# A two-block network on one core: bias tables at tile 9, the shift's chunks in another ring, and the mixers' matmuls of 128 and of 64 rows in separate groups

## The chip, the cores and the metric

The kernel runs on one core of one Trainium2 chip, as one program launch. The metric is the device time of that launch in microseconds (us); runs are summed up by their median. The engines are TensorE (PE in the profile; its weight loads are PEld), VectorE (DVE), ScalarE (ACT), GpSimd (POOL) and SyncE (SP), whose queue issues nearly all DMAs, strictly in order.

## The reference, cut to what matters

The input is 256 tokens of width 1024, all in float32. The first block runs two layers. Each layer is

```
mod = (silu(c) @ ada_w[l] + ada_b[l]).reshape(B, 3, 3, 1, D)       # shift, scale, gate of three sublayers
h = rms_norm(x, g0) * (1 + scale0) + shift0
x = x + 0.5 * gate0 * swiglu(h, ffn1_w13[l], ffn1_w2[l])           # width 2816
h = rms_norm(x, g1) * (1 + scale1) + shift1
x = x + gate1 * (four mixers of width 256 on h @ w_in[l] + b_in[l], joined, @ w_out[l])
x = x + 0.5 * gate2 * swiglu(rms_norm(x, g2) * (1 + scale2) + shift2, ffn2_w13[l], ffn2_w2[l])
```

The four mixers are a sparse attention (with a table of relative position biases, `t5_table`), a short convolution, a gated delta rule and an mLSTM. The last two work in chunks of 64 tokens. For the delta rule, with state S of each of four heads,

```
v_new = u_c - w_c @ S
o     = qd_c @ S + qk_c @ v_new
S     = S * gt_c + kd_c.T @ v_new
```

and for the mLSTM the output is a sum of `q_c @ C` (the state) and `s @ v_c` (inside the chunk), divided by a normaliser. A second block of two layers (a recurrent and attention mixer, a retention mixer, and two wide MLPs) follows; the change does not touch it.

## The kernel before, in words

Every large weight lies in one DRAM stream, cut into chunks of 128 rows by 1024 columns (512 KB). `raw` (L135) loads a chunk with one DMA on SP's queue into a ring of buffers; `weights` (L153) then splits it into a rounded part `whi` on ScalarE (L150) and a remainder `wlo` on VectorE or GpSimd (L151), and each product is three fp32r matmuls (L167 to L169). The weights' ring `wraw` has four buffers, `whi` and `wlo` four each, so loads can run about four feature tiles' halves ahead of the splits and those about as far ahead of TensorE.

The Tile framework decides the order of instructions on each engine by simulating the program's timeline at build time; an instruction may be placed earlier than its place in the text. Two things pin the order. `tc.issue_after(x)` puts an instruction behind `x` on its engine; and while `self.in_order` is set, `raw` pins each load behind the last SP instruction of the text, so that SP issues in the order of the text. `in_order` holds in the first FFN from its beginning through its last feature tile.

The first FFN of the first layer, `ffn` (L368) with `begin` (L2220) and `side` (L2336), goes like this:

- `begin` handles feature tiles 0 to 5 together ("wide": eight steps over k, each with a column of x scaled by `mod`), then tiles 6 and 7, one product for each half z. The wide chunks and those of tiles 6 and 7 use the ring `g` of 16 places. The scale vector's eight chunks of the modulation weights are loaded into the ring `wada` (three buffers) and reduced on VectorE (`ada_parts`, L233: one multiply and sum over 1024 columns, then a small correction). The shift vector's eight chunks are loaded by `shift_part` (L2253), also into `wada`, and reduced on TensorE by narrow matmuls (`strips`, L252). Four further steps of `ada_parts` are taken by `next(more)` (L2297), one for each half of tiles 6 and 7.
- The loop over tiles 8 to 21 loads two chunks for each tile, multiplies, scales by `rstd` (`se`, L384), applies SiLU and the gate (`sb`, L392), splits the result into `g` (L150 on ScalarE, L151 on GpSimd), and takes one step of `ada_parts`, which loads one chunk and reduces it.
- From tile `SIDE` (12) on, each tile also takes a step of `side`: first four loads (1104 KB of constants, an identity of 64 KB, a one-hot table of 49.5 KB and the bias table), four matmuls of 33 rows into the two PSUM banks that the shift's sums also use, and four ScalarE copies that make `bv` (`bias_tables`, L463, L474, L475); a tile later `skew` (L477) stores `bv` to DRAM on SP (L484); two tiles later it loads it back skewed as `bt` (L487); two tiles later VectorE copies parts of it to `bc` (L494). These SP instructions are pinned into the order of the text.
- The second product of the FFN runs over eight output tiles m, each in three cuts of k (`W2_CUTS`, 24 chunks in all). At the head of each m it takes two steps of `ada_parts`. There, SP is no longer pinned, and no VectorE instruction of `ada_parts` is pinned anywhere.

In the mixers, a planner (`weave`, L521) interleaves the streams of the four mixers and the output product by start times and paces. In `gdn` (L835), each of four chunks computes for each head `qd @ S` (L981, 128 rows: a state of two heads' width, padded with zeros) and `Qm @ v_new` (L982, 64 rows) into one PSUM tile, head after head. In `mlstm` (L1018), each half t computes for each head and chunk `qT @ C` into `pa` (L1141, 128 rows) and `sT @ v1` into `pb` (L1143, 64 rows), in turn. Each of these fp32 matmuls is two records in the trace.

Of the kernel before, what the change touches and what calls it, by code (L numbers as in the profile page):

```python
# [12 lines left out]
ALU = mybir.AluOpType  # L13
# [15 lines left out]
WIDE = 6  # L29
FIRST = 8  # L30
PLACES = 16
SIDE = 12
W2_CUTS = ((0, 8), (8, 15), (15, 22))


# [136 lines left out]
class Block1(Core):  # L172
# [50 lines left out]
    def ada_parts(self, pool, rows, name="wada", bufs=3):  # L223

        nc = self.nc
        for l, j in rows:
            t = self.mod[l, j] = self.keep1.tile([P, 8], F32, name=f"mod{l}_{j}")
            o = self.col_at[f"adab{l}"][0] + 8 * j
            s, kind = divmod(j, 3)
            for m in range(8):  # L230
                w = self.raw(f"ada{l}_{j}_{m}", pool, name, bufs)
                c, b = t[:, m:m + 1], self.cols[:, o + m:o + m + 1]
                nc.vector.scalar_tensor_tensor(w, w, 1.0, self.cond, op0=ALU.mult, op1=ALU.mult, accum_out=c)  # L233
                if kind == 1:
                    g = self.col(f"g{l}_{s}")
                    if m == 0:

                        bg = pool.tile([P, 8], F32, name="bg", bufs=2)
                        nc.vector.scalar_tensor_tensor(bg, self.cols[:, o:o + 8], 1.0, g, op0=ALU.add, op1=ALU.mult)
                    nc.vector.scalar_tensor_tensor(c, c, g[:, m:m + 1], bg[:, m:m + 1], op0=ALU.mult, op1=ALU.add)  # L240
                elif kind == 2 and s != 1:
                    nc.vector.tensor_scalar(c, c, b, 0.5, op0=ALU.add, op1=ALU.mult)
                else:
                    nc.vector.tensor_tensor(c, c, b, op=ALU.add)
                yield
# [122 lines left out]
    def ffn(self, l, s, ada1, ada2, begin=None, side=None):  # L368
        nc, tc = self.nc, self.tc
        psum = Banks(self.pp, acc="bbccdd", st="xy", acc2="ddy", late="dd")  # L370
        with tc.tile_pool(name=f"fh{l}_{s}", bufs=1) as hp:
# [26 lines left out]
            if begin:  # L398

                m0 = FIRST  # L400
                self.in_order = True
                steps = self.ada_parts(hp, ada1 + ada2)
                late, extra = begin(psum, hp, steps)
                self.in_parts = True
                sides = side(psum, hp)
            else:
                steps = self.ada(hp, ada1)
# [33 lines left out]
            self.h = [(a[:, 0:TN], b[:, 0:TN]) for a, b in zip(*([v[:, k] for k in range(KD)] for v in (self.vhi, self.vlo)))]  # L441
            for m in range(KD):
                ps = psum.tile([P, T], F32, name="acc2", bufs=3)
                if begin:
                    for _ in range(2):
                        next(steps, None)
                else:
                    for _ in ada2:
                        next(steps)
                for k0, k1 in W2_CUTS:  # L450
                    w = self.weights(f"w2_{l}_{s}_{m}_{k0}")
                    for k in range(k0, k1):
                        self.mm(ps, w, g[k], slice((k - k0) * P, (k - k0 + 1) * P), k == 0, k == FT - 1)
                self.add_out(m, ps, self.mod[l, 3 * s + 2], (l, 1) if s == 0 else (1, 0) if l == 0 else None)
                if begin and m == 5:

                    hi, lo = self.early
                    self.split(self.mod[l, 3][:, :, None].to_broadcast([P, KD, 2]), hi[:, :, T:], lo[:, :, T:])
# [18 lines left out]
    def skew(self, dr):  # L477


        nc = self.nc  # L480
        self.bt = self.keep1.tile([P, 4, T], F32, name="bt")
        self.bc = self.keep1.tile([P, 2, 4, 16], F32, name="bc")
        d = dr.tile([P, 4, 384], F32, name="bdram")
        nc.sync.dma_start(d, self.bv)  # L484
        yield
        yield
        nc.sync.dma_start(self.bt, bass.AP(tensor=d.tensor, offset=d.offset + 127, ap=[[1535, P], [384, 4], [1, T]]))  # L487
        nc.gpsimd.memset(self.bc, NEG)
        yield
        yield  # L490
        for t in range(2):
            n = 7 if t == 0 else 15
            o = 31 + 128 * (1 - t)
            nc.vector.tensor_copy(self.bc[:, t, :, 0:n], self.bt[:, :, o:o + 16 * (n - 1) + 1:16])  # L494
# [340 lines left out]
    def gdn(self):  # L835
# [129 lines left out]
        for ck in range(4):  # L965
            t, q = divmod(ck, 2)
            s = slice(64 * q, 64 * q + 64)
            tk = slice(64 * ck, 64 * ck + 64)
            if ck:
                ps = big([P, 4, 64])  # L970
                for hh in range(4):
                    nc.tensor.matmul(ps[s, hh], wT[hh % 2][:, t, q, hh // 2], S[:, hh // 2], start=True, stop=True)
                nc.vector.tensor_tensor(vn[s, t], u[s, t], ps[s], op=ALU.subtract)
                vc = vn
            else:
                vc = u
            yield
            ps = big([P, 4, 64])
            for hh in range(4):
                if ck:  # L980
                    nc.tensor.matmul(ps[s, hh], qd[hh % 2][:, hh // 2, tk], S[:, hh // 2], start=True, stop=False)  # L981
                nc.tensor.matmul(ps[s, hh], Qm[s, t, hh], vc[s, t, hh], start=not ck, stop=True)  # L982
            nc.scalar.activation(o[s, t], ps[s], AF.Copy)
            if ck == 3:
                break
            ps = big([P, 2, 64])
            for hh in range(4):
                z = slice(64 * (hh % 2), 64 * (hh % 2) + 64)
                nc.tensor.matmul(ps[z, hh // 2], kd[s, t, hh], vc[s, t, hh], start=True, stop=True)
            Sn = self.mx.tile([P, 2, 64], F32, name="cS", bufs=2)  # L990
            if ck:
                for f in range(2):
                    nc.vector.scalar_tensor_tensor(Sn[:, f], S[:, f], eg[:, f, 64 * ck + 63:64 * ck + 64], ps[:, f],
                                                   op0=ALU.mult, op1=ALU.add)
            else:
                nc.vector.tensor_copy(Sn, ps)
            S = Sn
            yield
# [19 lines left out]
    def mlstm(self):  # L1018
# [115 lines left out]
        for t in range(2):  # L1134
            pa = big([P, 4, 65])
            pb = big([P, 4, 65])
            for hh in range(4):
                for q in range(2):
                    s = slice(64 * q, 64 * q + 64)
                    tk = slice(t * P + 64 * q, t * P + 64 * q + 64)  # L1140
                    nc.tensor.matmul(pa[s, hh], qT[hh % 2][:, hh // 2, tk], C[:, 2 * t + q, hh // 2],  # L1141
                                     start=True, stop=True)
                    nc.tensor.matmul(pb[s, hh], sT[s, t, hh], v1[s, t, hh], start=True, stop=True)  # L1143
            yield
            n1 = self.mx.tile([P, 4, 65], F32, name="dn1", bufs=1)
# [1068 lines left out]
def first(b, z_ap, c_ap, t5_ap, onehot_ap, cst_ap, where):  # L2214
    nc, tc = b.nc, b.tc
    with ExitStack() as ctx:
        b.open1(ctx)
        dr = ctx.enter_context(tc.tile_pool(name="bd", bufs=1, space=DRAM))

        def begin(psum, pool, more):  # L2220

            b.condition(c_ap)
            steps = b.ada_parts(pool, [(0, 1)])
# [29 lines left out]
            def shift_part(h, q):  # L2253

                if q == 0:
                    sums[h] = psum.tile([P, 2, 256], F32, name="st")
                w = b.raw(f"ada0_0_{4 * h + q}", pool, "wada", 3)
                a = [w[:, k % 4 * 256:(k % 4 + 1) * 256] for k in range(KD)]
                b.strips(sums[h][:, q // 2], cond, a, range(4 * (q % 2), 4 * (q % 2) + 4))

# [29 lines left out]
            for m in range(WIDE, FIRST):  # L2290
                t = pool.tile([P, 2, T], F32, name="se2", bufs=FIRST)
                for z in range(2):
# [1 line left out]
                    ps = psum.tile([P, T], F32, name="acc")  # L2294
                    b.product(ps, b.weights(f"w13_0_0_{m}_{z}", False, raws[-1]), [(a[:, 0:T], c[:, 0:T]) for a, c in b.u])
                    nc.vector.tensor_tensor(t[:, z], ps, b.rstd, op=ALU.mult)
                    next(more)  # L2297
                    if m == WIDE and z == 0:
                        finish(0)
                    for q in ((0,), (1,), (2, 3), ())[2 * (m - WIDE) + z]:  # L2300
# [35 lines left out]
        def side(psum, pool):  # L2336
            nc.sync.dma_start(b.ident, b.ident_ap)
            b.constants1(cst_ap, where)
            b.bias_tables(t5_ap, onehot_ap, psum, pool)
            yield  # L2340
            yield from b.skew(dr)

        for l in range(2):
# [64 lines left out]
```

## Time and profile before

| what | value |
|---|---|
| three runs | 1999.63, 1990.77, 1995.83 us; median 1995.83 us |
| profiled execution | 2000.48 us, its span 1998.6 us, mean granted clock 0.975 |
| TensorE, weight loads | 96 % and 91 % of the span |
| VectorE, ScalarE, GpSimd | 75 %, 51 %, 28 % of the span |
| chain that ended last | TensorE 85 %, VectorE 7 %, DMA 3 % |
| DMA | 384.21 MB, mean 192 GB/s |

The first block takes the first 1100 us or so of the span: the first FFN of layer 0 from 0 to 245, its mixers from there to 455, the second FFN to 850, and the mixers of layer 1 to about 1050. A row of the timeline gives the start, the length, the engine, the source line and what is written from what; rows of the same kind are merged, with their count as x2 and so on, and a bracket gives the idle time before and what ended it. A matmul's length covers its fill and drain and overlaps the next one, so a rate is read from the distance of starts. PEclk is the clock that TensorE was granted: 1.00 is 2.4 GHz and 0.50 is 1.2 GHz, and a figure between is a mixture over the stretch.

### The profile page before, as it was taken

To read this page: it belongs to the slowest core of one execution; us is meant where nothing else is said; L and a number is where in the kernel's file an instruction comes from. 1 tells how busy PE (TensorE), PEld (TensorE's weight loads), DVE (VectorE), ACT (ScalarE), POOL (GpSimd) and SP (SyncE) were. 2 spreads that over 40 slices of the span, in tenths; PEclk is the share of its full clock that TensorE was granted. 3 is DMA by queue.
4 is the path that set the end of the run, shared out by engine and by line. 5 is a ranking of instruction groups with operands and counts; after the bars stand their busy time and mean duration, and the time that the engine had idled before them with its cause. 6 is when DMAs were issued, how large, how long until landed. Compare 5 with 4: busy or idle time off the path is not lost.

```text
span 1998.6 us, 40143 instructions
## 1 busy us (share of the span) xinstructions
PE 1926.8 (96%) x16031; PEld 1827.9 (91%) x16031; DVE 1501.9 (75%) x2693; ACT 1009.7 (51%) x1712; POOL 566.0 (28%) x474
## 2 busy tenths in 40 slices
PE   7989988999999999989999999999999999999998
PEld 7889977889999999977889999878999999999998
DVE  7669688678997999987547665678985686568954
ACT  4445454345454555454335554565654465556643
POOL 1143341104431443351104440313421122243302
PEclk9999988999999999989989999989999999999999
DMA  8758648326787788845116766424455544446562
GB/s 332 271 218 316 209 131 261 109 87 240 286 279 259 264 287 280 304 142 176 63 35 210 221 189 194 142 80 136 159 190 166 194 131 156 150 158 195 174 202 95
DMA packets 108808, 384.21 MB, mean 192 GB/s; under 512 B 12075, under 2 KB 14668, under 8 KB 108364
## 3 DMA queue, kind: packets, MB, share of 16 engines
q1 hardware_dynamic: 108620, 381.64, 57.0%
q8 instruction: 126, 2.06, 0.4%
q14 instruction: 62, 0.51, 0.1%
HBM read 379.76 MB, written 1.84 MB: 191 GB/s over the span
## 4 chain that ended last, share of the span: by engine, by line
PE 85%; DVE 7%; DMA 3%; issue 2%; ACT 1%; POOL 1%; SPq 0%; POOLq 0%; ACTq 0%; DVEq 0%
PE acc L167 23%; PE acc L169 23%; PE acc L168 23%; DMA wraw<-in_stream_dram 2%; DVE wlo L151 1%; PE b L2007 1%; DVE wada L233 1%; PE pa L1284 1%; ACT whi L150 1%; PE pc L924 1%; PE pa L1311 1%; DVE vlo L292 1%; DMA g<-in_stream_dram 1%; PE pc L942 1%; PE acc L733 1%
## 5 line engine op out<-in xcount | busy, mean ns | idle before, releaser
L150 ACT ACTIVATE whi<-wraw 128x1024 fp32r<-128x1024 f32 (+2 forms) x546 | 563.5, 1036 | 466.3 <-PE acc L168 323.9
L151 DVE TENSOR_TENSOR wlo<-wraw,whi 128x1024 fp32r<-128x1024 f32 (+1 forms) x471 | 594.9, 1266 | 204.1 <-ACT whi L150 197.5
L167 PE MATMUL acc<-vhi,whi 128*128 128x258 f32 (+3 forms) x2176 | 621.7, 288 | 21.2 <-ACT whi L150 17.6
L168 PE MATMUL acc<-vlo,whi 128*128 128x258 f32 (+3 forms) x2176 | 620.8, 286 | 2.4 <-DVE vlo L292 2.4
L169 PE MATMUL acc<-vhi,wlo 128*128 128x258 f32 (+3 forms) x2176 | 615.6, 286 | 3.1 <-DVE wlo L151 3.0
L167 PEld LDWEIGHTS acc<-vhi,whi 128*128 128x128 f32 x2176 | 413.1, 191 | 28.9 <-ACT whi L150 19.5
L168 PEld LDWEIGHTS acc<-vlo,whi 128*128 128x128 f32 x2176 | 416.0, 191 | 5.3 <-DVE vlo L292 3.2
L169 PEld LDWEIGHTS acc<-vhi,wlo 128*128 128x128 f32 x2176 | 411.6, 190 | 6.9 <-DVE wlo L151 4.0
L151 POOL TENSOR_TENSOR wlo<-wraw,whi 128x1024 fp32r<-128x1024 f32 (+1 forms) x75 | 190.2, 2540 | 271.2 <-ACT whi L150 261.3
L168 PE MATMUL acc<-g,whi 128*128 128x256 f32 x704 | 199.2, 283 | 0.8 <-POOL g L151 0.8
L167 PE MATMUL acc<-g,whi 128*128 128x256 f32 x704 | 198.4, 282 | 1.3 <-ACT g L150 1.3
L169 PE MATMUL acc<-g,wlo 128*128 128x256 f32 x704 | 199.1, 283 | 0.0
L167 PE MATMUL acc<-hhi,whi 128*128 128x256 f32 (+1 forms) x576 | 169.7, 298 | 6.4 <-ACT whi L150 2.8
L169 PE MATMUL acc<-hhi,wlo 128*128 128x256 f32 (+1 forms) x576 | 168.7, 295 | 0.0
L168 PE MATMUL acc<-hlo,whi 128*128 128x256 f32 (+1 forms) x576 | 168.3, 293 | 0.0
L151 POOL TENSOR_TENSOR g<-sb,g 128x256 fp32r<-128x256 f32 x88 | 106.1, 1209 | 161.7 <-ACT g L150 150.5
L167 PE MATMUL acc<-ghi,whi 128*128 128x272 f32 (+1 forms) x512 | 146.4, 286 | 0.0
L169 PE MATMUL acc<-ghi,wlo 128*128 128x272 f32 (+1 forms) x512 | 145.9, 285 | 0.0
L168 PE MATMUL acc<-glo,whi 128*128 128x272 f32 (+1 forms) x512 | 145.7, 285 | 0.0
L167 PEld LDWEIGHTS acc<-g,whi 128*128 128x128 f32 x704 | 133.5, 190 | 1.5 <-ACT g L150 1.5
L168 PEld LDWEIGHTS acc<-g,whi 128*128 128x128 f32 x704 | 133.1, 189 | 1.0 <-POOL g L151 1.0
L169 PEld LDWEIGHTS acc<-g,wlo 128*128 128x128 f32 x704 | 133.2, 189 | 0.0
(631 smaller groups left out, 3610.9 us busy)
## 6 DMA issues: line engine op xcount, KB each, us to landing
wraw<-in_stream_dram SPq DMA_DIRECT2D x502, 512.0 KB, 4.0
wada<-in_stream_dram SPq DMA_DIRECT2D x128, 512.0 KB, 4.7
wraw<-in_stream_dram SPq DMA_DIRECT2D x64, 448.0 KB, 4.5
g<-in_stream_dram SPq DMA_DIRECT2D x16, 512.0 KB, 7.5
wraw<-in_stream_dram SPq DMA_DIRECT2D x8, 384.0 KB, 3.1
cst<-in_cst_dram SPq DMA_DIRECT2D x1, 1104.0 KB, 7.9
z<-in_z_dram SPq DMA_DIRECT2D x8, 136.0 KB, 6.9
rows<-in_rows_dram SPq DMA_DIRECT2D x2, 532.0 KB, 4.7
```

What stands on the lines that cost most here:

```text
L150: self.nc.scalar.activation(hi, src, AF.Copy)
L151: (self.nc.gpsimd if pool else self.nc.vector).tensor_tensor(lo, src, hi.bitcast(F32), op=ALU.subtract)
L167: nc.tensor.matmul(ps, wh[:, kw], xh, start=start, stop=False)
L168: nc.tensor.matmul(ps, wh[:, kw], xl, start=False, stop=False)
L169: nc.tensor.matmul(ps, wl[:, kw], xh, start=False, stop=stop)
L233: nc.vector.scalar_tensor_tensor(w, w, 1.0, self.cond, op0=ALU.mult, op1=ALU.mult, accum_out=c)
L292: nc.vector.scalar_tensor_tensor(lo[:, m, 0:T], self.x[m], A[:, m:m + 1], hi[:, m, 0:T].bitcast(F32), op0=ALU.mult, op1=ALU.subtract)
L733: nc.tensor.matmul(ps[t], hh[:, tk], wh[:, kw], start=k == 0, stop=False)
L924: nc.tensor.matmul(ps[s, hh], M[s, t, hh], c["eye"][s] if v == 1 else de[t][s, 0, hh], start=True, stop=True)
L942: nc.tensor.matmul(ps[s, 1, hh], p1[t][s, hh], de[t][s, 1, hh], start=True, stop=True)
L1284: nc.tensor.matmul(ps[:, 0:n], qn[z, hh // 2, t * P:(t + 1) * P], keys[b, hh % 2][:, 0:n], start=True, stop=True)
L1311: nc.tensor.matmul(ps[:, hh], PT[hh][:, kb], v[:, kb, b], start=kb == 0, stop=kb == t)
```

## The change

Six edits, in three groups.

1. Bias tables: `SIDE` becomes 9. `side` waits four tiles between making the tables and storing them, so the store stands at tile 13 as before; the load back stands at tile 14 instead of 15, and the copies to `bc` at tile 18 instead of 17.
2. Modulation: the shift's eight chunks are loaded into the ring `wraw` instead of `wada`. The four steps at tiles 6 and 7 go; the second product takes 18 steps instead of 14, one ahead of each cut but the first of an m (and one ahead of that too for m = 2 and 5) instead of two at the head of each m. While `in_parts` is set (tile 8 to the end of the FFN), the VectorE reduction of a step is pinned behind the last VectorE instruction of the text.
3. Mixers: `gdn` issues the four heads' `qd @ S` first and then the four `Qm @ v_new`, with one start and one stop for the bank; `mlstm` issues all eight `qT @ C` and then all eight `sT @ v1`.

```diff
-SIDE = 12
+SIDE = 9
@@ ada_parts
-                nc.vector.scalar_tensor_tensor(w, w, 1.0, self.cond, op0=ALU.mult, op1=ALU.mult, accum_out=c)
+                with self.tc.issue_after(self.last(mybir.EngineType.DVE)) if self.in_parts else ExitStack():
+                    nc.vector.scalar_tensor_tensor(w, w, 1.0, self.cond, op0=ALU.mult, op1=ALU.mult, accum_out=c)
@@ ffn
-                late, extra = begin(psum, hp, steps)
+                late, extra = begin(psum, hp)
@@ ffn, second product
-                if begin:
-                    for _ in range(2):
+                for _ in () if begin else ada2:
+                    next(steps)
+                for k0, k1 in W2_CUTS:
+                    if begin and (k0 or m in (2, 5)):
                         next(steps, None)
-                else:
-                    for _ in ada2:
-                        next(steps)
-                for k0, k1 in W2_CUTS:
                     w = self.weights(f"w2_{l}_{s}_{m}_{k0}")
@@ skew
         nc.sync.dma_start(d, self.bv)
         yield
-        yield
         nc.sync.dma_start(self.bt, bass.AP(tensor=d.tensor, offset=d.offset + 127, ap=[[1535, P], [384, 4], [1, T]]))
         nc.gpsimd.memset(self.bc, NEG)
-        yield
-        yield
+        for _ in range(4):
+            yield
@@ gdn
             ps = big([P, 4, 64])
+            for hh in range(4) if ck else ():
+                nc.tensor.matmul(ps[s, hh], qd[hh % 2][:, hh // 2, tk], S[:, hh // 2], start=hh == 0, stop=False)
             for hh in range(4):
-                if ck:
-                    nc.tensor.matmul(ps[s, hh], qd[hh % 2][:, hh // 2, tk], S[:, hh // 2], start=True, stop=False)
-                nc.tensor.matmul(ps[s, hh], Qm[s, t, hh], vc[s, t, hh], start=not ck, stop=True)
+                nc.tensor.matmul(ps[s, hh], Qm[s, t, hh], vc[s, t, hh], start=not ck, stop=not ck or hh == 3)
@@ mlstm
                     nc.tensor.matmul(pa[s, hh], qT[hh % 2][:, hh // 2, tk], C[:, 2 * t + q, hh // 2],
                                      start=True, stop=True)
+            for hh in range(4):
+                for q in range(2):
+                    s = slice(64 * q, 64 * q + 64)
                     nc.tensor.matmul(pb[s, hh], sT[s, t, hh], v1[s, t, hh], start=True, stop=True)
@@ begin, shift_part
-                w = b.raw(f"ada0_0_{4 * h + q}", pool, "wada", 3)
+                w = b.raw(f"ada0_0_{4 * h + q}", b.wp, "wraw", WRAW)
@@ begin, tiles 6 and 7
-                    next(more)
@@ side
             b.bias_tables(t5_ap, onehot_ap, psum, pool)
-            yield
+            for _ in range(4):
+                yield
             yield from b.skew(dr)
```

## Rows read from the trace of the kernel before

**Rows 1.** The page, busy time of each engine.
```profile
PE 1926.8 (96%) x16031; PEld 1827.9 (91%) x16031; DVE 1501.9 (75%) x2693; ACT 1009.7 (51%) x1712; POOL 566.0 (28%) x474
```

**Rows 2.** Windows: PE, PEld, DVE, ACT, POOL busy (records), PEclk, DMA share, GB/s.
```profile
70.00:80.00 10.00, 10.00 (x60) 7.72 (x61) 6.85 (x13) 5.20 (x7) 0.45 (x1) 0.72 0.95 370
...
120.00:130.00 10.00, 4.32 (x27) 3.45 (x26) 3.65 (x8) 3.58 (x8) 1.40 (x2) 0.84 0.79 286
130.00:140.00 10.00, 9.54 (x68) 9.36 (x68) 9.39 (x14) 5.08 (x8) 2.39 (x1) 0.82 1.04 403
...
150.00:160.00 10.00, 10.00 (x86) 10.00 (x85) 9.94 (x15) 5.02 (x11) 6.84 (x4) 1.00 0.80 291
...
180.00:190.00 10.00, 7.90 (x58) 7.49 (x57) 10.00 (x18) 6.59 (x11) 2.87 (x2) 0.91 0.91 303
190.00:200.00 10.00, 10.00 (x79) 10.00 (x79) 9.37 (x18) 4.78 (x8) 0.27 (x1) 0.92 1.00 385
```

**Rows 3.** Waits of SP's DMA queue, 0 to 130: total us, times, longest.
```profile
SPq L484 <- ACT bv L475: 22.4, 1, 22.4
...
SPq L140 <- PE st L252: 16.6, 6, 5.8
```

**Rows 4.** Timeline of SP's queue: start us, us, line, tile, count.
```profile
61.05 0.43 SPq L140 DMA_DIRECT2D g<-in_stream_dram  x1
...
92.39 6.54 SPq L140 DMA_DIRECT2D wraw<-in_stream_dram  x2
121.43 0.33 SPq L484 DMA_DIRECT2D bdram<-bv  x1
...
125.70 0.38 SPq L487 DMA_DIRECT2D bt<-bdram  x1
```

**Rows 5.** Timeline of PE where it waited in the first FFN.
```profile
68.03 0.39 PE L167 MATMUL acc<-vhi,whi 128*128 128x256 f32 x1 [1.48 <-ACT whi L150]
...
129.38 0.58 PE L167 MATMUL acc<-vhi,whi 128*128 128x258 f32 x1 [5.68 <-ACT whi L150]
```

**Rows 6.** Timeline of DVE at the FFN's second product.
```profile
185.80 0.47 DVE L392 SCALAR_TENSOR_TENSOR sb<-se,sh 128x256 f32<-128x256 f32 x1
```

**Rows 7.** DVE's groups by form, 178 to 246: count, busy us, mean ns, idle before.
```profile
L151 DVE TENSOR_TENSOR wlo<-wraw,whi 128x896 fp32r<-128x896 f32 x16 | 18.4, 1153 | 7.2 <-ACT whi L150 7.1
L233 DVE SCALAR_TENSOR_TENSOR wada<-wada,cond 128x1024 f32<-128x1024 f32 x12 | 15.1, 1257 | 0.0
...
L292 DVE SCALAR_TENSOR_TENSOR vlo<-z,mod,vhi 128x256 fp32r<-128x256 f32 x7 | 6.6, 945 | 0.9 <-ACT vhi L291 0.9
```

**Rows 8.** Timeline of PE in layer 0's mixers.
```profile
415.28 0.69 PE L1141 MATMUL pd<-dC,dqT 128*64 128x65 f32 x16
...
421.29 0.68 PE L972 MATMUL pc<-cS,cwT 128*64 128x64 f32 x8
...
422.96 0.68 PE L1143 MATMUL pd<-dv,dsT 64*64 64x65 f32 x16
...
425.05 0.33 PE L982 MATMUL pc<-cvn,csegi 64*64 64x64 f32 x2
425.30 0.33 PE L981 MATMUL pc<-cS,cqd 128*64 128x64 f32 x2
```

**Rows 9.** PE in layer 1's mixers: timeline; windows of both layers, as rows 2.
```profile
1009.83 0.33 PE L1141 MATMUL pd<-dC,dqT 128*64 128x65 f32 x2
...
400.00:450.00 50.00, 49.98 (x530) 42.86 (x530) 35.21 (x101) 24.32 (x63) 2.50 (x3) 1.00 0.29 88
...
1014.30:1031.50 17.20, 17.20 (x103) 14.03 (x102) 6.33 (x24) 4.40 (x12) 1.00 (x1) 0.50 0.01 1
```

**Rows 10.** Groups by form of DVE and POOL, 130 to 178, columns as rows 7.
```profile
L392 DVE SCALAR_TENSOR_TENSOR sb<-se,sh 128x256 f32<-128x256 f32 x6 | 7.0, 1168 | 0.3 <-ACT sh L421 0.3
...
L151 POOL TENSOR_TENSOR wlo<-wraw,whi 128x1024 fp32r<-128x1024 f32 x4 | 12.3, 3085 | 7.8 <-ACT whi L150 7.7
L151 POOL TENSOR_TENSOR g<-sb,g 128x256 fp32r<-128x256 f32 x8 | 11.8, 1489 | 17.2 <-ACT sh L421 11.2 <-ACT g L150 6.0
```

More of the change, by code (lines that the diff above doesn't have):

```diff
@@ L2218, in first, with begin @@
         dr = ctx.enter_context(tc.tile_pool(name="bd", bufs=1, space=DRAM))
-        def begin(psum, pool, more):
+        def begin(psum, pool):
             b.condition(c_ap)
```

## The prediction

> **What bounds the kernel now.** I read the page first: TensorE is busy 96% of the span and nothing else comes near [rows 1]. So a microsecond counts only where TensorE waits, or runs at its lower clock, or takes longer for a matmul than it must. Next I read the windows of the first FFN, since four of the six edits are there. Three stretches stand out [rows 2]: 70 to 80 has a granted clock of 0.72, 120 to 140 has 5.7 us of idle TensorE and clocks of 0.84 and 0.82, and 180 to 200 has 2.1 us of idle and 0.91 and 0.92. Then the waits of SP's queue over the same time [rows 3]: one wait of 22.4 us, the bias tables' store for the copies that make `bv`, and 16.6 us in six waits for the strips' matmuls (L252), which free the places of the shift's chunks. The timelines of SP and TensorE tie these to the stalls [rows 4, 5]. Last I read TensorE in both mixers for what matmuls of 128 and of 64 rows cost side by side [rows 8, 9].
>
> **The change part by part.**
>
> Shift's chunks in `wraw` (A). Before, a shift chunk holds a place of `wada` until TensorE has run its strips, and the next load of that ring, with all that stands behind it on SP, waits. Tile 7's last weights stand behind such a wait and are issued at 61.05 [rows 4]; TensorE idles 1.48 us for them until 68.03 [rows 5]. Then the clock is low: 0.72 over 10 us is 5.6 us at 1.2 GHz and the rest at 2.4, and in those 5.6 half the work, 2.8 us, is lost. In the new text the only waits of this kind ahead of tile 8 are those of the last four shift chunks for the strips of the first four, which TensorE runs long before; the four wada loads of tiles 6 and 7 are gone as well. A is 1.5 + 2.8 = 4.3. What is late next: tile 8's and 9's loads now wait for the strips of the last four chunks, which TensorE must run ahead of tile 8 anyway. Bounds 0 (such a load takes the place of the stall) to 5.
>
> Bias tables (B). SP issues tile 13's weights by 98.9 and then stands at the store until 121.43 [rows 4], with every later weight load behind it. TensorE lives on its lead of 16.7 us (22.4 less the idle 5.68), stops at 123.70 and waits until 129.38 [rows 5]. Idle 5.7; 0.82 in 130 to 140 is 3.6 us at the low level, 1.8 lost; 0.7 for the slow start before 130 and the 0.46 of idle behind it. B is 8.2. In the new text the tables come behind tile 9. Tiles 10 to 13 are 48 matmuls each, 5.8 us at some 0.12 (86 in 10 us at full clock [rows 2]), and the tables themselves some 4 us, so tile 9 ended at about 123.7 - 23 - 4 = 96 to 97, and `bv` is ready between 98 and 104 in old times: SP waits 0 to 6 us, well inside the lead. The moved step issues the same four loads, four matmuls and four ScalarE copies three tiles earlier; on SP its 1.2 MB pass ahead of the weights of tiles 10 to 12, of which TensorE needs the first some 20 us later. The load back stands one tile behind the store, which took at most 4.3 us to land (121.43 to 125.70); that wait too lies inside the lead. At tile 9 the tables share two banks with the late shift columns; with nothing placed between, TensorE would wait up to 4 us. Bounds 4 to 9.
>
> Steps in the second product (C). From 180 to 190 VectorE is busy without a gap [rows 2], because reductions belonging to the second product's heads are placed early; so the last tile's `sb` runs only at 185.80 [rows 6], and TensorE loses 2.1 of idle, and by 0.91 and 0.92 3.4 us at the low level, 1.7. Pinned in the text's order, those reductions no longer pass `sb`: +3.8. Against that, the second product has 18 steps instead of 14. Its sum on VectorE [rows 7]: 24 x 1.15 for `wlo`, 18 x (1.26 + 0.2 of small ones), 8 x 0.95 for `vlo`, 8 updates of x at 0.47 (an operation of the form and size of rows 6) are 65 us, while TensorE's 8 x 22 x 3 matmuls are 62 to 64 at some 0.12. VectorE is at the bound there, and I charge 2.3. C is 1.5, bounds -7 to 4. In rows 7 `vlo` takes 0.95 where the like-sized `sb` of rows 6 takes 0.47; `wlo` is hardly stretched. The Trainium skill, "SBUF — State Buffer", Who interferes with whom, says why it can be worse: a VectorE instruction with two SBUF inputs and a GpSimd one that reads SBUF shut each other out for a whole instruction. By the row the sum is 65; if by the rule each of the eight `vlo` waited for a whole GpSimd instruction of 1.5 us [rows 10] it would be some 8 us more and C about -6, an estimate that the bounds hold.
>
> Delta rule (D). In turn, a block of two records starts every 0.26 us (425.05 to 425.30); eight such blocks a chunk are 2.06. In one group, eight records of 128 rows take 0.68 at most, and sixteen of 64 rows 0.68, so eight take 0.4 [rows 8]; together 1.08. Part of the first block stands apart already. I take 0.8 a chunk; three chunks in two layers give 4.9, bounds 2.5 to 5.8.
>
> mLSTM (E). In layer 0 the timeline shows L1141 and L1143 in groups already [rows 8]: nothing to win. In layer 1 the first half alternates sixteen blocks from 1009.83 on [rows 9], 4.1 us at 0.26 each; in two groups 0.69 + 0.68 = 1.4. E is 2.75, bounds 0 to 3.
>
> The clock behind it (F). Right behind that alternation, the granted clock is 0.50 from 1014.3 to 1031.5 while TensorE never idles [rows 9]; at most half of it, 8.6 us, is lost. In layer 0, where the same steps run in groups, the clock is 1.00 from 400 to 450 [rows 9]. I take 4, bounds -7 (a fall in layer 0 instead) to 8.6.
>
> The sum is 4.3 + 8.2 + 1.5 + 4.9 + 2.75 + 4 = 25.7, say 26 us. Against the profiled execution's 2000.5 that is 1974.3. That execution lies 4.7 above the median of the runs, so the forecast is 1995.8 - 26 = 1970.
>
> **The rivals.**
>
> VectorE gives part of it back. The second product is VectorE's: if its 24 `wlo` and 18 steps wait for each other as pinned and their sum grows from 65 to 74 (each of them stretched by a fifth of a microsecond), TensorE waits 11 there: 1996 - (26 - 1.5) + 11 = 1982. For: rows 7. Against: loads and splits run ahead, and 7 us of VectorE's idle there were waits for ScalarE.
>
> The regrouping doesn't do what it says. The order is placed anew, and layer 0 shows that it departs from the text: L1143 was moved apart there. If the placement splits the groups again, or what is saved only exposes VectorE's chains in the mixers, D, E and F are nothing: 1996 - 14 = 1982. Against: TensorE does not idle in either stretch.
>
> Slower: VectorE falls behind in tiles 8 to 21. A reduction pinned behind `sb` can no longer fill VectorE's wait for ScalarE's SiLU. VectorE needs 1.5 `wlo` at 1.2, two `se` at 0.4, `sb` and a step, 4.6 us a tile, against TensorE's 5.8, but it is stretched by GpSimd: `sb` took 1.17 on average here, not 0.47 [rows 6, 10]. If all of GpSimd's 3 us a tile (1.49 and half of 3.09) blocked VectorE, a tile would be 7.6: 1.8 x 14 = 25 us, and the waits bring clock falls of 2.8 each (as behind 68.03, A), say seven: 20. 1996 - 25 + 45 = 2016. It decides from 5.8 us of VectorE a tile. Against: with that stretching, TensorE was busy 10.00 of 10 at 150 to 160 [rows 2]. The rule of the Trainium skill named under C is what would make this happen; for `sb` the trace agrees with it.
>
> **How the numbers follow.** The forecast has 0.63, the two partial ones 0.16 and 0.13, the slower one 0.08. About 0.5%, 10 us, is what a measurement of this kernel can tell from no change, so faster begins below 1986. Faster: 0.61 + 0.10 + 0.10 = 0.81; slower: 0.07; the rest, 0.12, lies within. The range runs from the sum of all upper bounds, 35 (1961), to the partial rivals at 1982, each widened by the spread of the runs, some 5 us to either side: 1955 to 1988. That leaves out the slower case and the edges, some 2 in 10.
>
> **What would show it.** A: no idle of TensorE and clock 1.00 from 60 to 80. B: SP's wait at the store under 6 us; no idle at tile 14. C: `sb` of tile 21 within 3 us of its matmuls, and no TensorE waits for `wlo` later in the second product. D, E: L981 in runs of eight records, L1141 of sixteen in both layers. F: clock 1.00 through layer 1's mLSTM. It is wrong if the mixers' clock falls elsewhere, or if TensorE waits for `wlo` from tile 8 on.

## The result, and the profile after

The changed kernel takes 1972.02 us (median of 7 runs, 1969.46 to 1983.29), the kernel before 1995.83 (7 runs, 1990.77 to 1999.63). The ratio is 0.9894, 95% interval 0.9868 to 0.9920, so faster, by some 21 us (24 by the medians). The forecast was 1970. The profiled execution took 1972.02 us itself, with a span of 1970.2. The total came out near the forecast; its parts did not, and most of what follows is about that.

Page of the changed kernel, busy time of each engine, as [rows 1]:

```profile
PE 1906.0 (97%) x16031; PEld 1811.7 (92%) x16031; DVE 1498.1 (76%) x2693; ACT 1009.2 (51%) x1712; POOL 566.2 (29%) x474
```

Windows of the changed kernel, columns as [rows 2]:

```profile
70.00:80.00 10.00, 10.00 (x65) 6.46 (x64) 4.16 (x4) 3.79 (x7) 2.39 (x1) 1.00 0.84 330
120.00:130.00 10.00, 10.00 (x86) 10.00 (x85) 9.69 (x15) 6.58 (x13) 8.87 (x5) 1.00 0.62 230
130.00:140.00 10.00, 10.00 (x86) 10.00 (x85) 7.94 (x12) 3.74 (x8) 4.52 (x3) 1.00 0.72 265
170.00:180.00 10.00, 8.11 (x65) 7.69 (x64) 9.70 (x18) 6.41 (x10) 2.41 (x2) 1.00 0.93 315
190.00:200.00 10.00, 10.00 (x86) 10.00 (x85) 10.00 (x16) 4.58 (x7) 1.67 (x2) 1.00 0.96 354
```

The stalls of 70 to 80 and 120 to 140 are gone, and the clock is full there. The idle time at the end of the first product is not gone: TensorE is busy 8.11 of 10 in 170 to 180, where the same place before had 7.90 [rows 2].

Waits and timeline of SP's queue, as [rows 3, 4]:

```profile
SPq L140 <- PE st L253: 23.3, 5, 7.5
SPq L483 <- ACT bv L474: 6.1, 1, 6.1
```

```profile
104.98 0.33 SPq L483 DMA_DIRECT2D bdram<-bv  x1
...
108.42 0.43 SPq L485 DMA_DIRECT2D bt<-bdram  x1
```

The store waits 6.1 us instead of 22.4, just above the 0 to 6 forecast, and the load back follows 3.4 us later. The strips still hold SP for 23.3 us, more than the 16.6 before, but TensorE no longer waits behind them.

TensorE in both layers' mixers, as [rows 8, 9]:

```profile
418.61 0.68 PE L970 MATMUL pc<-cS,cwT 128*64 128x64 f32 x8
419.13 0.63 PE L978 MATMUL pc<-cS,cqd 128*64 128x64 f32 x8
...
996.07 0.69 PE L1139 MATMUL pd<-dC,dqT 128*64 128x65 f32 x16
996.68 0.68 PE L1144 MATMUL pd<-dv,dsT 64*64 64x65 f32 x16
```

The groups are there: sixteen records and sixteen records where sixteen blocks of two took turns. From 985 to 1060 the granted clock is 1.00, with no stretch at 0.50.

One reading serves all that follows. Each run lists its time and its mean granted clock. Time times clock is the least that the run would have taken with the clock at its upper level throughout; the rest is what the low level cost at most, since idle time at the low level would not have shrunk. Before, 48 runs: 1951.2 and 42.3. After, 13 runs of two measurements: 1942.0 and 29.6. So 9.2 us of the gain are work or idle time that went, and 12.7 are clock. By the forecast's terms it should have been 15.4 and 10.3 (clock: 2.8 of A, 1.8 of B, 1.7 of C, 4 of F).

```
kernel                   runs  mean us  time x clock   rest
before                    48   1993.5   1951.2 +-0.3   42.3 +-0.8
FFN's four edits          12   1995.8   1950.0 +-1.1   45.8 +-2.3
delta rule alone          12   1984.6   1944.4 +-0.8   40.2 +-1.4
mLSTM alone               12   1985.5   1949.3 +-0.7   36.2 +-1.5
both mixers               13   1977.1   1942.9 +-0.5   34.2 +-0.8
all (after)               13   1971.6   1942.0 +-0.6   29.6 +-1.5
all but delta rule         4   1976.6   1946.4 +-1.5   30.1 +-1.5
all but mLSTM              4   1977.2   1947.5 +-0.9   29.7 +-0.8
all but early tables       4   1976.0   1940.9 +-1.3   35.1 +-1.3
all but wraw for shift     6   1973.2   1942.7 +-0.8   30.6 +-2.0
all, two steps later       4   1971.0   1940.9 +-1.3   30.1 +-3.1
the same, wlo behind sb    6   1969.8   1941.3 +-0.8   28.6 +-1.2
```

(+- is the standard error of the mean; runs on different chips stand together, and the means of the kernel before differ by up to 6 us from chip to chip.) "Lead" below is my own measure: how much earlier the same VectorE and ScalarE instructions start than in the profiled execution of before, as a median over the 25 us of before that begin at the time named.

### The profile page after: what moved, and what is told of

It is laid out like the page before. It is cut to its first block, busy times and chain, and to the rows that moved or that the text cites. A ratio compares the mean times of both kernels' runs of the same rounds, so it can differ in the third digit from the quotient of the medians.

```text
span 1970.2 us, 40148 instructions
## 1 busy us (share of the span) xinstructions
PE 1906.0 (97%) x16031; PEld 1811.7 (92%) x16031; DVE 1498.1 (76%) x2693; ACT 1009.2 (51%) x1712; POOL 566.2 (29%) x474
## 4 chain that ended last, share of the span: by engine, by line
PE 85%; DVE 8%; DMA 3%; issue 2%; ACT 2%; POOL 1%; POOLq 0%; SPq 0%; DVEq 0%; ACTq 0%
PE acc L167 24%; PE acc L169 23%; PE acc L168 23%; DMA wraw<-in_stream_dram 2%; DVE wlo L151 1%; PE b L2008 1%; DMA wada<-in_stream_dram 1%; PE pa L1285 1%; PE pc L922 1%; ACT whi L150 1%; DVE sb L393 1%; PE pa L1312 1%; PE s L1824 1%; PE pc L940 1%; PE acc L731 1%
```

## The experiments

**Which half carries the gain.** The first four kernels each do a part alone.

FFN's edits alone, the mixers as before:

```
-            for hh in range(4) if ck else ():
-                nc.tensor.matmul(... qd ... start=hh == 0, stop=False)
+                if ck:
+                    nc.tensor.matmul(... qd ... start=True, stop=False)
-            for hh in range(4):
-                for q in range(2):
-                    s = slice(64 * q, 64 * q + 64)
```

> The changed kernel with the old order of the matmuls in gdn and mlstm. Theory: the first FFN's edits and the mixers' edits are separate gains. The lead over the kernel before is 12 to 13 us at 300 us, stays there through layer 0's mixers (400 to 450 us lose nothing, since the loss of 1 us seen there in the changed kernel comes from the mixers' new order), and layer 1's mixers again alternate sixteen blocks and fall to the low clock: about 12.5 us faster than before, some 1983 against 1995. Rival: the loss in layer 0's mixers comes from the new first FFN, whose end shifts what the placement sees; then the lead sinks to about 8 at 375 here too. Second rival: the low clock of layer 1 is a matter of phase and goes away by the shift alone; then 20 us or more faster.

Measured: 1994.49 against 1992.12, ratio 1.0005 (0.9976 to 1.0033): nothing. The lead is 13.7 us at 300, as the theory had it, then 1.9 at 425; the theory's 1983 missed, and the rival named the place but too small a loss (8 left at 375). In layer 0 the placement now lets the mLSTM's matmuls of 128 and 64 rows take turns as well as the delta rule's, which did so before [rows 8]. TensorE's timeline of this kernel:

```profile
414.57 0.33 PE L1141 MATMUL pd<-dv,dsT 64*64 64x65 f32 x2
414.83 0.33 PE L1139 MATMUL pd<-dC,dqT 128*64 128x65 f32 x2
415.09 0.33 PE L1141 MATMUL pd<-dv,dsT 64*64 64x65 f32 x2
415.25 0.28 PE L980 MATMUL pc<-cvn,csegi 64*64 64x64 f32 x2
415.46 0.33 PE L979 MATMUL pc<-cS,cqd 128*64 128x64 f32 x2
415.72 0.32 PE L980 MATMUL pc<-cvn,csegi 64*64 64x64 f32 x2
```

and the window behind it:

```profile
415.00:436.00 21.00, 21.00 (x126) 17.00 (x125) 7.17 (x25) 4.26 (x13) 0.73 (x1) 0.59 0.00 1
```

TensorE is busy without a gap and its clock averages 0.59: 17 us of the 21 at the low level, 8.6 lost. The blocks start 0.16 to 0.26 us after the one ahead, most of them 0.26, as in [rows 8].

Both mixers' edits alone (the other half of the diff, put into the kernel before):

> The kernel before with only the two edits in the mixers. Theory: layer 1's mixers win 13 to 16 us (4 to 5 of alternation, about 8 of the low clock that does not come, the rest in the delta rule), layer 0's win 0 to 2.5: 13 to 17 us faster than before, some 1980. Granted clock 1.00 from 1000 to 1040. Rival: the clock falls there in any case, by what stands beside the mLSTM; then 7 to 8 us faster, some 1988.

Measured: 1975.91 against 1992.12, ratio 0.9903 (0.9871 to 0.9934), as the theory had it. Run again beside the changed kernel:

> The mixers' regroupings alone, beside the changed kernel on one chip: what the four edits in the first FFN add to them. Theory: the FFN's edits remove idle time of 1.5 and 5.7 us and what the low clock behind them costs, 12 us by the traces at 300, and that lasts to the end: 1984 to 1986 where the changed kernel has 1973, at a clock lower by 0.002. Rival: the FFN's edits are mostly given back, by clock falls that come elsewhere instead (the medians so far lie only 2 to 4 us apart): 1975 to 1978, with the same granted clock as the changed kernel within 0.001.

Measured: 1977.17 against 1991.94, ratio 0.9936 (0.9913 to 0.9960), where the changed kernel had 1969.27. Between theory and rival: the FFN's edits add 8 us to the mixers', not 12 and not 2 to 4.

The mLSTM's regrouping alone, and the delta rule's alone:

> The kernel before with only mlstm's two groups. Theory: the sixteen alternating blocks of layer 1 are what the clock falls for, so this alone wins 2.8 us of alternation and about 8 of clock: 10 to 11 us faster, some 1985, and layer 0 does not move. Rival: the delta rule's alternation behind it (1023 to 1026) keeps the clock low; then 3 to 5 us faster.

> The kernel before with only gdn's two groups. Theory: about 0.8 us for each of three chunks in two layers, 5 us, some 1990; the low clock of layer 1 at 1014 to 1031 stays, since the mLSTM's alternation ahead of it stays. Rival: the low clock goes; then 12 us faster. Second rival: the chain through VectorE sets the pace of the chunks and nothing is won.

Measured: 1984.96, ratio 0.9954 (0.9930 to 0.9978), and 1983.36, ratio 0.9955 (0.9935 to 0.9975), both against 1992.12. Each has half of what both have. For the mLSTM's alone the theory's time (1985) held, but layer 0 did move; for the delta rule's alone the time lies between the theory (5 us faster) and its first rival (12). They pay differently (table): the delta rule's takes 6.8 us off the time at full clock, the mLSTM's 1.9, but the mLSTM's takes 6.1 off the clock's rest. The profiled execution with the mLSTM's alone lost 11 us of lead in layer 0, at two falls of the clock, near 363 and 435; around the second the delta rule's blocks still take turns, at 429.54 to 431.1 and 436.5 to 439. These falls are not the edit's doing: up to 1010 us TensorE runs the same instructions in the same order as in the kernel before (VectorE and ScalarE throughout), and there the clock was 1.00 from 400 to 450 [rows 9]. Windows of it, and of layer 1 with the delta rule's alone, where the mLSTM's take turns from 1001.26 to 1006.9:

```profile
430.00:450.00 20.00, 20.00 (x129) 16.89 (x128) 6.05 (x20) 5.62 (x16) 0.73 (x1) 0.66 0.00 1
```

```profile
1000.00:1020.00 20.00, 20.00 (x157) 15.23 (x157) 9.59 (x30) 4.56 (x13) 1.60 (x2) 0.74 0.10 31
```

**The changed kernel again**, on one chip with the second measurement of both mixers, the shift's chunks in the old ring and the last kernel below.

> The changed kernel again, on the same chip as the three kernels it is to be compared with. Theory: about 1972 to 1975, mean granted clock 0.984; its lead over the profiled execution of before is 12.5 to 14.5 us at 300, falls by 3 to 5 at 350 and is back to 11 to 13.5 at 475, and layer 1's mixers bring 14 to 16 more between 1000 and 1100. Rival: the places were those of one execution, and the falls of the clock lie elsewhere in another; then the lead at 475 or the gain in layer 1 differs by more than 4 us.

Measured: 1969.27 against 1991.94, ratio 0.9890 (0.9862 to 0.9918). The lead is 10.5 at 300, 4.1 at 350, 10.5 at 475, a little under the theory, and goes from 11.3 to 27.1 in layer 1. The gain in layer 1 repeats to 0.1 us (15.8); from 300 to 425 the lead lies 2 to 4 us lower than in the first execution, and at 475 within 1. So what is read between 250 and 450 from one execution is good to some 4 us.

**Which regrouping keeps layer 0 in order.** All of the change but the delta rule's (`-start=hh == 0 +start=True`, Qm in the same loop again), and all but the mLSTM's (the two loops joined again):

> All of the change except the delta rule's regrouping. What it tells apart: which of the two regroupings keeps the first FFN's lead through layer 0's mixers. With neither (FFN edits alone) the lead fell from 13.7 us at 300 to 1.9 at 425 and the run ended level with before. Theory: layer 0 needs the delta rule's groups, because its blocks stand at the end of the mixer where the clock fell by half for 17 us without them; then this kernel's lead falls by 5 us or more between 300 and 475, layer 1 keeps the mLSTM's part, and the time is 1972 + 5 (three chunks in two layers at 0.8) + 5 to 8 (a low-clock stretch) = 1982 to 1985. Rival: either regrouping is enough to keep the rows of one kind together in layer 0; then only the 0.8 a chunk are lost and the time is 1975 to 1978, with no granted clock of 0.50 between 400 and 450.

> All of the change except the mLSTM's regrouping. Theory: in layer 0 the new placement lets the 128-row and the 64-row matmuls of the mLSTM alternate (sixteen blocks of 0.26 us against two groups of 0.69), 2.75 us; in layer 1 they alternate as before, 2.75 more, and the clock is 0.50 behind them for 10 to 17 us, 5 to 8.6 more: 1972 + 10.5 to 14 = 1982 to 1986. Rival: the gain of the mixers comes from the delta rule alone (its regrouping by itself measured 0.9955 of before) and the mLSTM's is worth only its 2.75 in layer 1: 1975.

Measured: 1976.24, ratio 0.9903 (0.9877 to 0.9930), and 1977.38, ratio 0.9910 (0.9886 to 0.9934), against 1995.32. For layer 0 the first one's rival holds: one regrouping is enough. The blocks of the other kind still take turns (L979 and L980 from 417.0 to 418.6 in the first, L1139 and L1141 from 411.5 to 412.8 in the second) and the clock stays full there. In layer 1 the second one's theory holds: the mLSTM's blocks take turns from 994.45 and the clock is 0.50 for 10 us from 995.9. Its time lies above the rival (1975) and below the theory (1982). Windows of the two in layer 0:

```profile
405.00:425.00 20.00, 20.00 (x193) 15.98 (x192) 10.91 (x38) 5.61 (x18) 0.73 (x1) 1.00 0.01 2
```

```profile
405.00:425.00 20.00, 20.00 (x210) 16.33 (x209) 11.47 (x40) 5.95 (x20) 0.95 (x2) 1.00 0.01 2
```

In time at full clock the delta rule's regrouping is worth 4.4 us here (standard error 1.6), the mLSTM's 5.5 (1.1). By the medians alone neither kernel could be told from the changed one.

**The bias tables late again.** `SIDE = 12`, store three and load two tiles behind, the rest as changed:

> The changed kernel with the bias tables where they were (behind tile 12, the store three and the load two tiles behind). Theory by the forecast: SP waits some 22 us at the store again, TensorE stops for 5.7 us at tile 14 and the clock falls behind it, so the lead over before drops by 8.2 at 130 to 150, to some 3 to 5 at 250, and the end is 1972 + 8.2 = 1980. Rival: what the first FFN wins is given back by the placement in layer 0's mixers anyway (FFN edits alone: 13.7 us at 300, 4.7 at 475, a time level with before); then most of the 8.2 is gone by 475 and the end is 1972 to 1976, as for the mixers' edits alone (1975.9).

Measured: 1975.59 against 1995.32, ratio 0.9901 (0.9877 to 0.9924). SP and TensorE wait as before:

```profile
SPq L483 <- ACT bv L474: 19.6, 1, 19.6
```

```profile
PE acc L167 <- ACT whi L150: 5.7, 1, 5.7
```

The lead at 175 is 2.3, where the changed kernel has 8.4 to 9.2, so the stall costs 6 to 7 in its place. TensorE itself has 8.7 there, by the last matmul of tile 21 in the changed kernel and in this one:

```profile
167.06 0.28 PE L169 MATMUL acc<-vhi,wlo 128*128 128x258 f32 x1
```

```profile
175.75 0.28 PE L169 MATMUL acc<-vhi,wlo 128*128 128x258 f32 x1
```

The last matmul of the second product starts at 239.25 here, at 232.81 and 234.31 in the changed kernel's two executions, so 4.9 to 6.4 are left there. At 300 the lead is 8.8 against 10.5 to 12.4, and at the end 1.5 to 3.0 are left. With the stall, TensorE is busy 10.00 of 10 in 170 to 180 and loses 1.4 us in the windows 325 to 375 and 400 to 450 together; without it, it loses 1.9 to 2.2 in the former and 3.7 to 3.8 in the latter. Windows of this kernel:

```profile
170.00:180.00 10.00, 10.00 (x86) 10.00 (x85) 8.77 (x19) 5.76 (x11) 1.97 (x2) 1.00 0.83 287
325.00:375.00 50.00, 48.60 (x489) 41.10 (x488) 32.53 (x74) 20.36 (x38) 4.55 (x5) 0.93 0.54 175
400.00:450.00 50.00, 50.00 (x542) 45.04 (x541) 36.24 (x103) 27.20 (x71) 8.22 (x7) 1.00 0.38 131
```

Theory (1980) missed, rival (1972 to 1976) held in time; but most of the loss comes ahead of 300, not in layer 0's mixers where the rival put it: the distance of the leads is 1.7 to 3.6 at 300 and 1.9 to 2.8 at 475.

**The shift's chunks in the old ring** (`b.wp, "wraw", WRAW` back to `pool, "wada", 3`):

> The changed kernel with the shift's chunks in the ring of wada as before. Theory by the forecast's first step, as the traces correct it: TensorE waits 1.5 us for tile 7's weights and the clock falls behind, so the lead over before at 80 is 0 instead of 2.5 and the whole lead to 300 is 2.5 to 3 lower; the end is 1975. Rival: TensorE's lead there is so thin that with the tables early a stall at tile 7 pushes the tables' store too, and more than 4 us are lost by 150; or, on the other side, nothing is lost at the end since the clock falls elsewhere anyway: 1972 to 1973.

Measured: 1971.34 against 1991.94, ratio 0.9916 (0.9885 to 0.9947), the changed kernel beside it 1969.27. TensorE idles once, for 0.6 us, and the clock stays at 1.00 from 60 to 80; the lead at 75 is 1.4 against 3.0. The ring is worth 1 to 2 us; theory (1975) missed. The stall of 1.48 is not there because this kernel undoes the ring alone: the four steps at tiles 6 and 7 are still gone, and SP issues tile 7's last chunk at 54.14, where it was 61.05 before [rows 4] and is 52.01 in the changed kernel.

**The late `sb`.** The steps of the last two tiles moved into the second product:

```
-                    next(steps)
+                    if m < FT - 2:
+                        next(steps)
-                    if begin and (k0 or m in (2, 5)):
+                    if begin and (k0 or m in (1, 2, 4, 5)):
```

> The changed kernel, with the two reduction steps of the first FFN's last two tiles moved into the second product (a second step in four of its heads). Theory: tile 21's sb waits for VectorE, which stands at a pinned step whose load has not landed; with those steps gone from there, sb follows its matmuls within 3 us and TensorE's idle of 1.9 us between 176 and 178 is gone, so the lead over before at 250 to 300 is 14 to 14.5 us instead of 12.5. The end is 1970, which only the trace can tell from 1972. Rival: the second product is VectorE's (10.00 of 10 busy at 190 to 220), so two more steps there, 1.46 each, come back as waits of TensorE for wlo: lead 10 to 12 at 250 to 300.

Measured: 1972.12 against 1995.32, ratio 0.9875 (0.9850 to 0.9901). `sb` of tile 21 runs at 174.60 instead of 175.50 and TensorE still idles 1.6 us; VectorE now stood 1.70 at a `wlo` ahead of `sb`. The theory missed. So that `wlo` was queued behind `sb` (`issue_after` the `sb` for the fourth `weights` of the second product):

> The changed kernel with the reduction steps of tiles 20 and 21 moved into the second product, and with the fourth wlo of the second product queued on VectorE behind tile 21's sb. Moving the steps alone brought sb forward by 0.9 us only, since VectorE then stood 1.7 us at that wlo for its whi from ScalarE. Theory: sb now starts when the SiLU is done, at 171 to 172.5 instead of 174.6, and TensorE's idle of 1.6 to 1.9 us between 170 and 180 is under 0.4; the time is 2 us below the changed kernel's on the same chip. Rival: g behind it is held up by ScalarE's whi copies and GpSimd's lower half, so the idle stays over 1 us; or VectorE, 10.00 of 10 busy from 200 on, takes it back and TensorE waits for wlo at 190 to 230.

Measured: 1969.14, beside 1969.27 for the changed kernel: no difference, and 1.8 us of idle. It missed too (the rival's first half held: over 1 us of idle, and ScalarE behind it), but it shows who holds `sb`. VectorE, then ScalarE, in this kernel:

```profile
175.79 0.48 DVE L393 SCALAR_TENSOR_TENSOR sb<-se,sh 128x256 f32<-128x256 f32 x1 [1.84 <-ACT sh L423]
```

```profile
172.74 0.51 ACT L391 ACTIVATE se<-se,sh 128x256 f32<-128x256 f32 x1
173.26 1.28 ACT L319 ACT_TABLE_LOAD   x1
174.56 1.06 ACT L150 ACTIVATE whi<-wraw 128x1024 fp32r<-128x1024 f32 x1
175.53 0.15 ACT L423 ACTIVATE sh<-acc 128x1 f32<-128x1 f32 x1
176.31 0.42 ACT L150 ACTIVATE g<-sb 128x256 fp32r<-128x256 f32 x1 [0.63 <-DVE sb L393]
```

`sb` needs two things from ScalarE: the SiLU (done at 173.25) and the second `sh`. Behind the last SiLU ScalarE loads another table and splits a weight tile before it copies that `sh` at 175.53: 2.3 us. In the changed kernel the same copy runs at 174.32, in the kernel before at 183.63, 2.2 us before its `sb` [rows 6]. The Trainium skill, "ScalarE: Activation LUTs", What ACT_TABLE_LOAD costs, gives some 1283 ns for the load; the row agrees. That `sh` copied ahead of the SiLU would end the wait was not tried.

## Why the prediction was right, and where it was not

**A, 4.3 forecast, 2.5 to 3 measured** (the lead at 75), of which the ring has 1 to 2. The mechanism held (no idle, clock 1.00 from 60 to 80), and most of it is the four steps that went: of the 9 us by which SP issues tile 7's last chunk earlier, they have 7 and the ring 2. The prediction had TensorE run the strips that SP waits for "long before"; SP waits for them longer than it did (23.3 us), without harm. The size was the loss in [rows 2] and [rows 5], taken from one execution. The five executions with the old FFN idle 1.5 to 2.4 us from 60 to 80, at a clock of 0.83 in the one that the prediction read, then 1.00, 0.91, 0.91 and 0.83: the idle time repeats, the clock does not.

**B, 8.2 forecast, 6 to 8.7 in its place, some 4 at the end.** Wait, lead and idle at tile 14 went as forecast. What failed is the assumption that the idle time stays gone. In time at full clock the early tables bring nothing that the runs can show (1942.0 with, 1940.9 without, with a standard error of 1.4 on the difference), only 5.5 of clock. Over the whole span (the page's span less TensorE's busy time) TensorE idles 64.2 and 67.1 us in the changed kernel's two executions and 69.7 with the tables late: of the 6.1 us of stall, 3 to 5 stay away. The rest comes back as idle time in two places: 1.9 and 2.2 at the end of the first product, where there is none with the tables late, and in layer 0's mixers. Windows there of the changed kernel run again, to be set beside those of the kernel with the tables late:

```profile
325.00:375.00 50.00, 46.43 (x510) 38.38 (x509) 35.86 (x82) 20.29 (x37) 4.70 (x5) 1.00 0.56 178
400.00:450.00 50.00, 49.73 (x521) 44.50 (x519) 36.09 (x105) 27.27 (x72) 8.58 (x7) 1.00 0.38 130
```

3.8 us of idle against 1.4. The eight profiled executions with the early tables lost 3.7 to 5.6 in these two windows, the six without them 0.1 to 2.9; the windows are fixed in time, so they do not hold quite the same work. TensorE waits there for ScalarE and VectorE, as in the changed kernel run again:

```profile
330.95 0.35 PE L167 MATMUL acc<-hhi,whi 128*128 128x256 f32 x1 [0.92 <-DVE dkT L644]
...
338.99 0.50 PE L731 MATMUL acc<-whi,hhi 128*128 128x512 f32 x1 [0.73 <-ACT dqT L650]
...
357.15 0.33 PE L1298 MATMUL pa<-ident,ap 128*128 128x128 f32 x1 [1.08 <-ACT ap L1290]
```

A further 3 us of the lead go between 250 and 300, where the clock was lower in the two executions of the changed kernel; the last section shows that this need not be a price of the edit. Against that, the kernel with the tables late had a fall of 7 us at 354. Without these two, the 8.7 less 2.3 to 3.8 by the end of the FFN less 2.4 in the mixers leave 2.5 to 4, an estimate from these three executions; the means of the runs have 4.4, with a standard error of 2.1.

The step that failed is the one that the prediction did not have: it priced each stall of the FFN in its own window and carried the sum unchanged through the end of the first product and through layer 0, whose order is placed anew by every edit ahead of it. The traces speak for the placement: from 255 to 400 us the kernel with the tables late, whose FFN is some 4 us shorter too, runs VectorE and ScalarE in the order of before and TensorE but for three matmuls, while the changed kernel's order differs on all three engines from about 322 of before's time. That the shorter FFN as such brings some of these waits is not excluded.

**C, 1.5 forecast, about 0 to 1.7.** "Those reductions no longer pass `sb`: +3.8" failed. They no longer pass it, yet `sb` is 8 us behind its matmuls as before, since ScalarE's queue holds it for 2.2 us and VectorE's `wlo` and steps, these now pinned ahead of it, fill the rest. The idle time is 1.9 (before 2.1). The clock behind it was 1.00 in one execution and 0.88 over 170 to 180 in the other. With the tables late TensorE comes to this point 8.7 us later and does not wait at all, so there the idle time went as forecast: it is TensorE's own lead that meets VectorE and ScalarE here. The charge of 2.3 for VectorE was not called for: it is busy 10.00 of 10 from 190 to 220 and TensorE does not wait.

**D, 4.9 forecast** (six times 0.8 is 4.8), **4.4 measured** as part of the change, 6.8 alone, with standard errors of 1.6 and 0.9. Right within that. The Trainium skill, "TensorEngine Tiling (Array Packing)", Tiling Modes, says that a change of tiling mode drains TensorE; the rows agree: 0.26 us for a block of two records in turn, 0.04 to 0.09 for a record in groups.

**E, 2.75 forecast, 5.5 measured** as part of the change, 1.9 alone. "In layer 0 nothing to win" was read from the order of before [rows 8]. For the order of before it was right: alone, the regrouping leaves layer 0's order as it was and brings 1.9 for the forecast 2.75. With the new FFN that order is another one, and without this edit layer 0 takes turns too, so it pays twice. E moves matmuls only, with their starts and stops unchanged, so for E it is the order that pays.

**F, 4 forecast, 8.1 measured.** The 17 us at 0.50 in layer 1 [rows 9] are gone and have come up nowhere else in that layer's mixers. It is not one execution's luck: of the fourteen profiled executions, the four without the mLSTM's regrouping all have this fall (17, 7, 10 and 10 us at 0.50, begun in the alternation or 0.3 us behind it), and the ten with it have none. What was a middle between -7 and 8.6 was the upper bound. With both regroupings the clock's rest falls from 42.3 to 34.2, with all edits to 29.6.

So FFN's part, 14 forecast, is 5.5 by the means on top of the mixers (8 by the medians on one chip), and nothing by itself; the mixers' part, 11.7 forecast, is 16. These are two errors of opposite sign, so it is in part luck that the median came out within 2 us of 1970; by the means of all runs the gain is 21.9 where 25.7 was forecast. Of the rivals, VectorE falling behind (2016) did not show: TensorE is busy 10.00 of 10 from tile 14 to 170. Giving back in the second product (1982) had the right idea in the wrong place: TensorE waits nowhere from 190 to 250. The regrouping did what it says.

## What to carry to other kernels

An idle stretch removed early in a kernel whose later order is placed by a program is only worth what is left of it behind the next stage: read the lead there, not where the stall was. Small matmuls of different row counts that take turns cost 0.26 us a block, and in the mLSTM's case here the clock too; group them in the text even where the placement happens to group them already, since the next edit changes the placement. With runs that each list their clock, time times clock has a smaller standard error than the time (0.3 for 0.8 us in 48 runs before, 1.1 for 1.9 in the twelve of the FFN's edits), and tells what is work from what is clock.

## What the runs showed of the hardware that I had not expected

The clock falls without an idle TensorE: 17 us at 0.50 behind [rows 9]'s alternation, 17 behind that of the FFN's edits alone in layer 0 and 7 in layer 1, 10 in layer 1 with the delta rule's regrouping alone and 10 there without the mLSTM's. For sixteen blocks of the mLSTM in layer 1 it came in four executions of four. Not every alternation is followed by one: none came in layer 0 of the two kernels with one regrouping undone, nor in layer 0 of the kernel before, where the delta rule's blocks take turns from 425 to 442. With the mLSTM's regrouping alone TensorE runs the same instructions in the same order there, and the clock fell for 14 us from 433. So for the delta rule's blocks one order has a fall in one execution and none in another; what decides stays open.

Executions of one kernel differ mostly in the clock: over the 48 runs of before the time has a standard deviation of 5.6 us, time times clock 2.4. Over 250 to 320 the two executions of the changed kernel had 0.80 and the one without the delta rule's regrouping 0.88, though TensorE, VectorE and ScalarE run the same instructions in the same order up to 408 us in both (the second execution of the changed kernel, then the other):

```profile
250.00:320.00 70.00, 55.47 (x410) 47.08 (x411) 55.77 (x124) 28.97 (x59) 23.25 (x17) 0.80 0.52 171
```

```profile
250.00:320.00 70.00, 54.25 (x430) 46.71 (x430) 57.97 (x127) 30.47 (x61) 28.11 (x18) 0.88 0.59 190
```

That is 27 and 17 us at the low level, 5 us of time at most, with no edit between them there. A clock fall read from one execution can be a draw, as here, or a price, as behind the mLSTM's blocks; only further executions tell which.
